# Reordering the pooling stage at the head of a two-layer trunk

## The chip, the cores and the metric

The kernel runs on one core of one Trainium2 chip. The metric is the device time of one launch in microseconds (us). The times shown of the kernel before are three runs: 983.19, 983.37 and 987.84 us, median 983.37. A profile is one execution, recorded by the chip's profiler. Its engines are PE (TensorE, matrix products), DVE (VectorE), ACT (ScalarE), POOL (GpSimd) and SP (SyncE, which here only issues DMAs).

## The reference

A decoder trunk of two layers on 512 tokens of width 1024, in float32:

```python
# layer 0: pooling mixer, layer 1: differential attention; each followed by a SwiGLU FFN
h = pool(x)                       # 4 groups of 256 columns, windows 2, 4, 8, 16
                                  # mixed = (mean over the last w tokens - x) @ w[g]; h = mixed * scale
x = LayerNorm(ALPHA * x + h)
x = LayerNorm(ALPHA * x + (silu(x @ w_gate) * (x @ w_up)) @ w_down)
```

`pool_w` is 4 x 256 x 256, `scale` has 1024 entries (one for each output column), `w_gate` and `w_up` are 1024 x 2816. The second layer does the same with attention in place of pooling. Only the first lines, the pooling mixer and its LayerNorm, are touched by the change.

## The kernel before

**Precision.** Float32 products are made of three faster ones: each operand is split in a high part (ACT casts it, L89) and a low part (DVE or POOL subtracts the cast from the original, L90), and `mm3` (L108 to L110) adds high x high, high x low and low x high in PSUM.

**Tiling.** The tokens are four blocks of 128. `res` holds x, a block in each of four column ranges; all sums and norms are made in it. The weights come as pieces of 128 x 1024 (512 KB) through a ring of four buffers `raw`; `fetch` issues their loads on SP's queue, `ready` splits them into `wh` and `wl` (rings of six). PSUM has eight banks, each a tile of 128 x 512.

**The pooling stage** (L217 to L402), in the order of the code:

1. Loads: the bands that pooling multiplies with (`bnd`, `d0`) on ACT's queue; x, the two pieces of pool weights, the scale row broadcast to 128 partitions (`sc`), the first FFN piece and small tables on SP's queue.
2. Nine warm-up matmuls on PE while x lands; then splits of x (`split_x`).
3. `low` pools blocks 0 and 1 into the banks of the first 256 tokens, `high` pools blocks 1, 2, 3 into those of the last 256. 40 and 48 matmuls of 256 columns.
4. `scale_weights` multiplies a piece of pool weights with `sc` (DVE, two instructions of 128 x 512), `pool_weights` splits it, `split_pooled` splits what was pooled, bank by bank.
5. `mixed(s)` multiplies block s with the pool weights (24 matmuls); `summed(s)` adds ALPHA * x and takes statistics (DVE: residual L145 and stats L152, twice); `spread_of` aggregates them (DVE, L158) and makes 1/sigma (POOL, two small instructions, L160 and L161); `norm` (DVE, L170) normalizes the block in place.
6. `turn(0, s)` transposes the block for the FFN: eight transposes on PE (L198), eight evictions on ACT with gain and bias (L203), two casts on ACT, and two low parts on DVE, whose row is `xt<-y,xt` at L90.

**Then the first FFN.** Its first two column tiles are computed for tokens 0 to 255 first (`g` and `u` products, 24 matmuls each), with `turn(0, 2)` and `turn(0, 3)` put in between, after the second and the third product; then for tokens 256 to 511.

**What sets the order.** The stage stands under `tc.manual_schedule()`. A helper's instructions are issued where it is called, each on the queue of its engine; the tile framework adds the semaphore waits and picks buffers.

Of the kernel before, what the change touches and what calls it, by code (L numbers as in the profile page):

```python
# [12 lines left out]
F32 = mybir.dt.float32  # L13
# [5 lines left out]
P = 128  # L19
S = 512  # L20
D = 1024
# [29 lines left out]
def trunk(ctx, tc, x, wall, pscale, lam_p, subln, table, lng, lnb, band, first, onehot, out):  # L51
    nc = tc.nc
# [5 lines left out]
    def bank(name):  # L58
        return ps.tile([P, 512], F32, tag="bank", name=name)
# [3 lines left out]
    def load_x(s):  # L63
        for d in range(2):
            c = slice(d * 512, (d + 1) * 512)
            nc.sync.dma_start(out=res[:, s, c], in_=x[s * P : (s + 1) * P, c])
# [8 lines left out]
    def fetch(upto):  # L75
        while fetched[0] < min(upto, total):
            c = fetched[0]
            raws[c] = keep.tile([P, 1024], F32, tag="raw", name=f"raw{c}", bufs=RAWS)
            nc.sync.dma_start(out=raws[c], in_=wall[c])
            fetched[0] += 1  # L80

    def split(dst_h, dst_l, src, scale=1.0, low=None):
        if scale != 1.0:
            nc.scalar.mul(dst_h, src, scale)
            nc.vector.scalar_tensor_tensor(
                dst_l, src, scale, dst_h.bitcast(F32), op0=ALU.mult, op1=ALU.subtract
            )
        else:
            nc.scalar.copy(dst_h, src)  # L89
            (low or nc.vector).tensor_tensor(dst_l, src, dst_h.bitcast(F32), op=ALU.subtract)  # L90

    def ready(upto, low=None):
        while divided[0] < min(upto, total):
            c = divided[0]
            fetch(c + RAWS)
            h = keep.tile([P, 1024], F32R, tag="wh", name=f"wh{c}", bufs=WBUFS)
            l = keep.tile([P, 1024], F32R, tag="wl", name=f"wl{c}", bufs=WBUFS)
            split(h, l, raws.pop(c), low=low)
            parts[c] = (h, l)
            divided[0] += 1  # L100
# [5 lines left out]
    def mm3(acc, a, b, start, stop):  # L106
        (ah, al), (bh, bl) = a, b
        nc.tensor.matmul(acc, ah, bh, start=start, stop=False)  # L108
        nc.tensor.matmul(acc, ah, bl, start=False, stop=False)  # L109
        nc.tensor.matmul(acc, al, bh, start=False, stop=stop)  # L110
# [81 lines left out]
    def turn(n, s):  # L192
        for i in range(2):
            pt = bank(f"pt{n}_{s}_{i}")
            y = keep.tile([P, 4, P], F32, tag="y", name=f"y{n}_{s}_{i}", bufs=2)
            for k in range(4):
                kk = 4 * i + k
                nc.tensor.transpose(  # L198
                    pt[:, k * P : (k + 1) * P], res[:, s, kk * P : (kk + 1) * P], ident
                )  # L200
            for k in range(4):
                kk = 4 * i + k
                nc.scalar.activation(  # L203
                    y[:, k, :],
                    pt[:, k * P : (k + 1) * P],
                    AF.Identity,
                    bias=bT[:, n, kk : kk + 1],
                    scale=gT[:, n, kk : kk + 1],
                )
            o = (s % 2) * P  # L210
            split(*(xt[:, s // 2, j, 4 * i : 4 * i + 4, o : o + P] for j in range(2)), y)
# [5 lines left out]
    with tc.tile_pool(name="pool", bufs=1) as pp:  # L217
        bnd = pp.tile([P, 4, 256], BF16, name="bnd")
        nc.scalar.dma_start(out=bnd, in_=band)
        d0 = pp.tile([16, 4, 16], F32, name="d0")  # L220
        nc.scalar.dma_start(out=d0, in_=first)
        for s in range(SB):
            load_x(s)
        fetch(1)
        sc = pp.tile([P, D], F32, name="sc")
        nc.sync.dma_start(out=sc, in_=pscale.broadcast_to([P, D]))
        fetch(3)
        tb = pp.tile([33, HEADS], F32, name="tb")
        nc.gpsimd.memset(tb, MASKED)
        nc.sync.dma_start(out=tb[:32, :], in_=table)  # L230
# [16 lines left out]
        def split_x(s, d, low=None):  # L247
            c = slice(d * 512, (d + 1) * 512)
            split(xnh[:, s, c], xnl[:, s, c], res[:, s, c], low=low)

        warm = bank("warm")
        for i in range(9):
            nc.tensor.matmul(warm[:, 0:P], ident, ident, start=True, stop=True)
        split_x(0, 0)
        nc.vector.tensor_copy(fh, bnd)
        split(fh[:16, :, 0:16], fl[:16, :, 0:16], d0)
# [2 lines left out]
        nc.scalar.copy(bh[:, :, P : 2 * P], bnd[:, :, :P])  # L259
        split_x(1, 1)  # L260
        nc.scalar.copy(bh[:, :, 2 * P : 3 * P], bnd[:, :, P:])
        ph = pp.tile([P, KB, S], F32R, name="ph")
        pl = pp.tile([P, KB, S], F32R, name="pl")
        pw = []

        def scale_weights(c):
            raw = raws[c]
            for j in range(2):
                r = raw[:, j * 512 : (j + 1) * 512].rearrange("p (k e) -> p k e", k=2)
                nc.vector.tensor_tensor(  # L270
                    r,
                    r,
                    sc[:, (2 * c + j) * GW : (2 * c + j + 1) * GW]
                    .unsqueeze(1)
                    .to_broadcast([P, 2, GW]),
                    op=ALU.mult,
                )

        def pool_weights(c):
            h = keep.tile([P, 1024], F32R, tag="wh", name=f"pwh{c}", bufs=WBUFS)  # L280
            l = keep.tile([P, 1024], F32R, tag="wl", name=f"pwl{c}", bufs=WBUFS)
            split(h, l, raws.pop(c))
            pw.append((h, l))
            divided[0] += 1
# [3 lines left out]
        def xk(t, s, k):  # L288
            return t[:, s, k * P : (k + 1) * P]
# [15 lines left out]
        def high(*blocks):  # L305
            for s in blocks:
                c = (3 - s) * P
                for k in range(KB):
                    g = k // 2
                    o = made[1, g][:, (k % 2) * 256 : (k % 2 + 1) * 256]  # L310
                    b = bh[:, g, c : c + 256]
                    mm(o, xk(xnh, s, k), b, start=s == 1 and k % 2 == 0, stop=False)
                    mm(o, xk(xnl, s, k), b, start=False, stop=s == 3 and k % 2 == 1)

        def split_pooled(half, *groups):
            for g in groups:
                c = slice(half * 256, (half + 1) * 256)
                split(
                    ph[:, 2 * g : 2 * g + 2, c],
                    pl[:, 2 * g : 2 * g + 2, c],  # L320
                    made[half, g].rearrange("p (k t) -> p k t", k=2),
                )

        def mixed(s):
            acc = [bank(f"mix{s}_{d}") for d in range(2)]
            for g in range(4):
                h, l = pw[g // 2]
                o = acc[g // 2][:, (g % 2) * GW : (g % 2 + 1) * GW]
                for k in range(2):
                    kk = 2 * g + k  # L330
                    c0 = (g % 2) * 512 + k * GW
                    mm3(
                        o,
                        (ph[:, kk, s * P : (s + 1) * P], pl[:, kk, s * P : (s + 1) * P]),
                        (h[:, c0 : c0 + GW], l[:, c0 : c0 + GW]),
                        k == 0,
                        k == 1,
                    )
            return acc
# [3 lines left out]
                residual(s, d, acc[d])  # L343
                stat(0, s, d)

        split_x(2, 0, nc.gpsimd)
        split_x(2, 1)
        split_x(3, 0, nc.gpsimd)
        split_x(3, 1)
        low(0, range(8))  # L350
        low(1, range(8))
        for g in range(4):
            made[1, g] = bank(f"pool1_{g}")
        high(1, 2)
        split_pooled(0, 0, 1)
        scale_weights(0)
        pool_weights(0)
        split_pooled(0, 2)
        scale_weights(1)
        pool_weights(1)  # L360
        split_pooled(0, 3)
        m0 = mixed(0)
        m1 = mixed(1)
        ready(3, nc.gpsimd)
        def lines_sum():
            b = [bank(f"line{i}") for i in range(2)]
            mm(b[0][:HEADS, :], tb, oh_[:, 0:512], start=True, stop=True)
            mm(b[1][:HEADS, :128], tb, oh_[:, 512:640], start=True, stop=True)
            return b

        high(3)
        summed(0, m0)
        spread_of(0, 0)
        split_pooled(1, 0, 1)
        norm(0, 0)
        ready(4, nc.gpsimd)
        summed(1, m1)
        spread_of(0, 1)
        split_pooled(1, 2, 3)
        norm(0, 1)  # L380
        turn(0, 0)
        b0, b1 = lines_sum()
        m2 = mixed(2)
        summed(2, m2)
        spread_of(0, 2)
        turn(0, 1)
        norm(0, 2)
        m3 = mixed(3)
        summed(3, m3)
        spread_of(0, 3)  # L390
        ready(5)
        norm(0, 3)
        ready(6)
        line = pp.tile([HEADS, LINE], F32, name="line")
        far = pp.tile([HEADS, 1], F32, name="far")
        nc.scalar.copy(far, b1[:HEADS, P - 1 : P])
# [682 lines left out]
```

## Time and profile before

| | us |
|---|---|
| median of three runs | 983.37 |
| profiled execution | 983.99 |
| its span | 982.1 |
| PE busy in the span | 960.4 |
| DVE / ACT / POOL busy | 641.3 / 418.3 / 120.4 |
| first pooling matmul starts | 6.96 |
| turn(0,0), turn(0,1) start on PE | 31.95, 37.09 |
| first FFN matmul starts | 40.84 |
| turn(0,2), turn(0,3) start on PE | 47.01, 50.76 |
| FFN's products for tokens 256 to 511 start | 54.51 |

How to read the rows. In a timeline a row is: start and duration in us, engine, line, operation, output<-inputs, shapes, xcount, and in brackets the idle time of the engine before it and what ended it. Merged rows show the start of the first and the time until the end of the last. Durations of PE's matmuls overlap: their starts are what counts. In the table by windows each row is: window, its length, then busy time and instruction count of PE, PEld (weight loads), DVE, ACT, POOL, then the clock that PE was granted (1.00 is full), the DMA engines' share and GB/s. A row of waits is: who waited, <- for whom, us in total, times, longest. A row of one tile's instructions gives the shortest, median and longest duration in ns and the first and last start. A row of DMA issues ends in KB and the median us from issue to landing.

### The profile page before, as it was taken

To read this page: it belongs to the slowest core of one execution; us is meant where nothing else is said; L and a number is where in the kernel's file an instruction comes from. 1 tells how busy PE (TensorE), PEld (TensorE's weight loads), DVE (VectorE), ACT (ScalarE), POOL (GpSimd) and SP (SyncE) were. 2 spreads that over 40 slices of the span, in tenths; PEclk is the share of its full clock that TensorE was granted. 3 is DMA by queue.
4 is the path that set the end of the run, shared out by engine and by line. 5 is a ranking of instruction groups with operands and counts; after the bars stand their busy time and mean duration, and the time that the engine had idled before them with its cause. 6 is when DMAs were issued, how large, how long until landed. Compare 5 with 4: busy or idle time off the path is not lost.

```text
span 982.1 us, 13302 instructions
## 1 busy us (share of the span) xinstructions
PE 960.4 (98%) x4922; PEld 815.5 (83%) x4922; DVE 641.3 (65%) x1007; ACT 418.3 (43%) x705; POOL 120.4 (12%) x192
## 2 busy tenths in 40 slices
PE   7999999999999999999999999999999999999995
PEld 6898888888888888988888888988888888888884
DVE  6756764455568577688777676756655555477687
ACT  4662222223326356656556554732223322245460
POOL 3301111111120211000000000011111111111102
PEclk8999999999999999999999999999999999999998
DMA  9266677655777975323232122276675666878842
GB/s 241 61 210 216 231 248 269 234 194 193 261 254 237 330 273 176 110 81 89 74 94 78 63 86 86 81 271 211 217 271 193 205 231 224 292 240 307 340 143 86
DMA packets 70221, 189.11 MB, mean 193 GB/s; under 512 B 15971, under 2 KB 16099, under 8 KB 70156
## 3 DMA queue, kind: packets, MB, share of 16 engines
q1 hardware_dynamic: 56556, 141.83, 43.0%
q0 software_dynamic: 13408, 46.15, 13.8%
q8 instruction: 39, 0.64, 0.3%
q10 hardware_dynamic: 192, 0.29, 0.1%
q14 instruction: 26, 0.21, 0.1%
HBM read 151.51 MB, written 36.72 MB: 192 GB/s over the span
## 4 chain that ended last, share of the span: by engine, by line
PE 86%; issue 5%; DVE 3%; ACT 2%; POOL 1%; DMA 1%; POOLq 0%; DVEq 0%
PE P L605 11%; PE g L109 8%; PE u L108 8%; PE u L109 8%; PE u L110 8%; PE g L108 8%; PE g L110 8%; PE Q L605 3%; PE s L790 2%; PE v L108 2%; PE v L109 2%; PE v L110 2%; PE wo L108 2%; PE wo L109 2%; PE wo L110 2%
## 5 line engine op out<-in xcount | busy, mean ns | idle before, releaser
L90 DVE TENSOR_TENSOR wl<-raw,wh 128x1024 fp32r<-128x1024 f32 x118 | 141.8, 1220 | 33.3 <-ACT wh L89 33.3
L89 ACT CAST wh<-raw 128x1024 fp32r<-128x1024 f32 x120 | 123.5, 1049 | 66.8 <-PE u L109 66.3
L109 PE MATMUL g<-xt,wh 128*128 128x512 f32 (+1 forms) x384 | 143.1, 373 | 0.5 <-DVE xt L90 0.3
L108 PE MATMUL g<-xt,wh 128*128 128x512 f32 (+1 forms) x384 | 143.0, 372 | 0.0
L108 PE MATMUL u<-xt,wh 128*128 128x512 f32 (+1 forms) x384 | 142.8, 372 | 0.0
L109 PE MATMUL u<-xt,wh 128*128 128x512 f32 (+1 forms) x384 | 142.8, 372 | 0.0
L110 PE MATMUL u<-xt,wl 128*128 128x512 f32 (+1 forms) x384 | 142.8, 372 | 0.0
L110 PE MATMUL g<-xt,wl 128*128 128x512 f32 (+1 forms) x384 | 142.7, 372 | 0.0
L436 DVE TENSOR_TENSOR hid<-sg,u 128x512 f32<-128x512 f32 x44 | 30.2, 687 | 155.8 <-PE u L110 153.5
L90 DVE TENSOR_TENSOR dl<-r,dh 128x1024 fp32r<-128x1024 f32 x84 | 94.2, 1132 | 39.9 <-ACT dh L89 39.5
L89 ACT CAST dh<-r 128x1024 fp32r<-128x1024 f32 x84 | 81.4, 979 | 71.7 <-PE P L605 31.2
L605 PE MATMUL P<-dh,xt 128*128 128x512 f32 x352 | 109.6, 390 | 0.0
L109 PEld LDWEIGHTS g<-xt,wh 128*128 128x128 f32 x384 | 72.3, 188 | 13.2 <-DVE xt L90 0.9
L110 PEld LDWEIGHTS u<-xt,wl 128*128 128x128 f32 x384 | 72.4, 189 | 12.5
L108 PEld LDWEIGHTS u<-xt,wh 128*128 128x128 f32 x384 | 72.4, 189 | 12.4
L110 PEld LDWEIGHTS g<-xt,wl 128*128 128x128 f32 x384 | 72.3, 188 | 12.5
L109 PEld LDWEIGHTS u<-xt,wh 128*128 128x128 f32 x384 | 72.4, 189 | 12.3
L108 PEld LDWEIGHTS g<-xt,wh 128*128 128x128 f32 x384 | 72.3, 188 | 12.4
L480 ACT CAST v<-u 128x512 fp32r<-128x512 f32 x22 | 13.6, 620 | 160.8 <-issue 151.1
L605 PEld LDWEIGHTS P<-dh,xt 128*128 128x128 f32 x352 | 66.1, 188 | 13.9 <-issue 0.2
L460 DVE TENSOR_TENSOR b<-b,b 128x512 f32<-128x512 f32 x88 | 60.8, 691 | 17.3 <-DMA b<-in_wall 15.2
L435 ACT ACTIVATE sg<-g 128x512 f32<-128x512 f32 x44 | 26.3, 598 | 101.0 <-PE g L110 99.3
(179 smaller groups left out, 1775.6 us busy)
## 6 DMA issues: line engine op xcount, KB each, us to landing
raw<-in_wall SPq DMA_DIRECT2D x128, 512.0 KB, 4.3
b<-in_wall SPq DMA_DIRECT2D x88, 256.0 KB, 5.6
tsum<-b POOLq DMA_DIRECT2D x88, 256.0 KB, 5.1
r<-tsum SPq DMA_DIRECT2D x40, 512.0 KB, 4.7
r<-in_wall SPq DMA_DIRECT2D x30, 512.0 KB, 4.7
ssum<-v POOLq DMA_DIRECT2D x22, 512.0 KB, 4.1
xt<-ssum POOLq DMA_DIRECT2D x20, 512.0 KB, 6.1
res<-in_x SPq DMA_DIRECT2D x8, 256.0 KB, 4.3
```

Source lines behind the costliest of these rows:

```text
L89: nc.scalar.copy(dst_h, src)
L90: (low or nc.vector).tensor_tensor(dst_l, src, dst_h.bitcast(F32), op=ALU.subtract)
L108: nc.tensor.matmul(acc, ah, bh, start=start, stop=False)
L109: nc.tensor.matmul(acc, ah, bl, start=False, stop=False)
L110: nc.tensor.matmul(acc, al, bh, start=False, stop=stop)
L435: nc.scalar.activation(sg, pg, AF.Silu)
L436: nc.vector.tensor_tensor(hid[:, f, :], sg, pu, op=ALU.mult)
L460: nc.vector.tensor_tensor(z, x, y, op=ALU.add)
L480: nc.scalar.copy(v[:, :, 0, :], u)
L605: nc.tensor.matmul(accs[s], x[:, k, r], y[:, c], start=first and k == 0 and e == 0, stop=last and k == m - 1 and e == 2, skip_group_check= ...
L790: nc.tensor.matmul(accs[c][:, :wide], a[r, qs], b[r, :wide], start=i == 0, stop=i == 2)
```

## The change

All of it is in the pooling stage.

- The scale row is loaded once (4 KB, on ACT's queue) and no longer broadcast by a DMA; two matmuls with a row of ones (`one`, set by POOL) spread it over 128 partitions in two banks, and ACT copies these into `sc`. Four of the nine warm-up matmuls go.
- The first FFN piece is fetched right behind the pool weights.
- POOL multiplies the pool weights with the scales; the low parts of blocks 2 and 3 that POOL made are made by DVE.
- `high` runs for blocks 1, 2, 3 in one stretch, ahead of all mixing; half of `split_pooled(1)` moves in front of the second pool weights' split, `ready(4)` stands in front of mixing.
- `turn(0, 0)` and the sums of the lines stand ahead of `mixed(2)` and of `summed(1)`; `turn(0, 1)` ahead of `summed(2)` and `mixed(3)`; `ready(5)` ahead of `norm(0, 1)`, `ready(6)` ahead of `norm(0, 3)`.

```diff
--- before.py
+++ after.py
@@ -217,14 +217,16 @@
     with tc.tile_pool(name="pool", bufs=1) as pp:
         bnd = pp.tile([P, 4, 256], BF16, name="bnd")
         nc.scalar.dma_start(out=bnd, in_=band)
+        scrow = pp.tile([1, D], F32, name="scrow")
+        nc.scalar.dma_start(out=scrow, in_=pscale)
         d0 = pp.tile([16, 4, 16], F32, name="d0")
         nc.scalar.dma_start(out=d0, in_=first)
         for s in range(SB):
             load_x(s)
-        fetch(1)
+        fetch(3)
         sc = pp.tile([P, D], F32, name="sc")
-        nc.sync.dma_start(out=sc, in_=pscale.broadcast_to([P, D]))
-        fetch(3)
+        one = pp.tile([1, P], F32, name="one")
+        nc.gpsimd.memset(one, 1.0)
         tb = pp.tile([33, HEADS], F32, name="tb")
         nc.gpsimd.memset(tb, MASKED)
         nc.sync.dma_start(out=tb[:32, :], in_=table)
@@ -249,8 +251,13 @@
             split(xnh[:, s, c], xnl[:, s, c], res[:, s, c], low=low)
 
         warm = bank("warm")
-        for i in range(9):
+        for i in range(5):
             nc.tensor.matmul(warm[:, 0:P], ident, ident, start=True, stop=True)
+        scb = [bank(f"sc{c}") for c in range(2)]
+        for c in range(2):
+            nc.tensor.matmul(
+                scb[c], one, scrow[:, c * 512 : (c + 1) * 512], start=True, stop=True
+            )
         split_x(0, 0)
         nc.vector.tensor_copy(fh, bnd)
         split(fh[:16, :, 0:16], fl[:16, :, 0:16], d0)
@@ -259,6 +266,8 @@
         nc.scalar.copy(bh[:, :, P : 2 * P], bnd[:, :, :P])
         split_x(1, 1)
         nc.scalar.copy(bh[:, :, 2 * P : 3 * P], bnd[:, :, P:])
+        for c in range(2):
+            nc.scalar.copy(sc[:, c * 512 : (c + 1) * 512], scb[c])
         ph = pp.tile([P, KB, S], F32R, name="ph")
         pl = pp.tile([P, KB, S], F32R, name="pl")
         pw = []
@@ -267,7 +276,7 @@
             raw = raws[c]
             for j in range(2):
                 r = raw[:, j * 512 : (j + 1) * 512].rearrange("p (k e) -> p k e", k=2)
-                nc.vector.tensor_tensor(
+                nc.gpsimd.tensor_tensor(
                     r,
                     r,
                     sc[:, (2 * c + j) * GW : (2 * c + j + 1) * GW]
@@ -343,54 +352,50 @@
                 residual(s, d, acc[d])
                 stat(0, s, d)
 
-        split_x(2, 0, nc.gpsimd)
-        split_x(2, 1)
-        split_x(3, 0, nc.gpsimd)
-        split_x(3, 1)
+        for i in range(4):
+            split_x(2 + i // 2, i % 2)
         low(0, range(8))
         low(1, range(8))
         for g in range(4):
             made[1, g] = bank(f"pool1_{g}")
-        high(1, 2)
-        split_pooled(0, 0, 1)
+        high(1, 2, 3)
         scale_weights(0)
+        scale_weights(1)
+        split_pooled(0, 0, 1, 2, 3)
         pool_weights(0)
-        split_pooled(0, 2)
-        scale_weights(1)
+        split_pooled(1, 0, 1)
         pool_weights(1)
-        split_pooled(0, 3)
-        m0 = mixed(0)
-        m1 = mixed(1)
         ready(3, nc.gpsimd)
+        ready(4, nc.gpsimd)
+
         def lines_sum():
             b = [bank(f"line{i}") for i in range(2)]
             mm(b[0][:HEADS, :], tb, oh_[:, 0:512], start=True, stop=True)
             mm(b[1][:HEADS, :128], tb, oh_[:, 512:640], start=True, stop=True)
             return b
 
-        high(3)
+        m0 = mixed(0)
+        m1 = mixed(1)
         summed(0, m0)
         spread_of(0, 0)
-        split_pooled(1, 0, 1)
+        split_pooled(1, 2, 3)
         norm(0, 0)
-        ready(4, nc.gpsimd)
+        b0, b1 = lines_sum()
+        turn(0, 0)
+        m2 = mixed(2)
         summed(1, m1)
         spread_of(0, 1)
-        split_pooled(1, 2, 3)
+        ready(5)
         norm(0, 1)
-        turn(0, 0)
-        b0, b1 = lines_sum()
-        m2 = mixed(2)
+        turn(0, 1)
         summed(2, m2)
         spread_of(0, 2)
-        turn(0, 1)
+        m3 = mixed(3)
         norm(0, 2)
-        m3 = mixed(3)
         summed(3, m3)
         spread_of(0, 3)
-        ready(5)
+        ready(6)
         norm(0, 3)
-        ready(6)
         line = pp.tile([HEADS, LINE], F32, name="line")
         far = pp.tile([HEADS, 1], F32, name="far")
         nc.scalar.copy(far, b1[:HEADS, P - 1 : P])
```

## The prediction

> **What bounds the kernel now.** Read first: the page's busy times, then PE's windows, then who waited for whom. All positions are us from the span's start.
>
> ```profile
> PE 960.4 (98%) x4922; PEld 815.5 (83%) x4922; DVE 641.3 (65%) x1007; ACT 418.3 (43%) x705; POOL 120.4 (12%) x192
> ```
>
> ```profile
> 6.96:15.70 8.74, 8.74 (x72) 8.58 (x72) 7.31 (x10) 5.59 (x11) 3.00 (x2) 1.00 1.11 332
> 15.70:18.46 2.76, 0.55 (x3) 0.19 (x1) 1.65 (x3) 1.53 (x2) 0.00 (x0) 1.00 0.87 11
> 18.46:28.50 10.04, 8.44 (x47) 7.85 (x48) 6.46 (x10) 2.48 (x3) 3.17 (x3) 0.66 0.77 210
> ...
> 30.40:31.95 1.55, 0.16 (x3) 0.03 (x1) 1.55 (x4) 1.55 (x3) 0.68 (x1) 1.00 0.00 0
> 31.95:40.84 8.89, 8.89 (x69) 7.82 (x69) 8.69 (x16) 7.45 (x20) 2.97 (x4) 1.00 0.18 61
> 40.84:54.51 13.67, 13.53 (x115) 13.33 (x113) 9.45 (x14) 10.71 (x25) 2.65 (x4) 1.00 0.44 154
> ```
>
> PE is 98% busy, so a change ahead of the first FFN can only move the moment at which PE's unbroken run begins. It begins at 31.95: from there PE is busy in 8.89 of 8.89 and 13.53 of 13.67. Before it PE stands 2.2 in 15.70:18.46, about 1.6 in 18.46:28.50 (which also ran at a granted clock of 0.66), and 1.4 in 30.40:31.95. Those stalls are all that a better order can win.
>
> ```profile
> ACT ph L89 <- PE pool L313: 6.5, 1, 6.5
> ```
>
> The third block's pooling stands behind two blocks of mixing, so ACT waits 6.5 for it, and DVE's norm and PE's first turn (pt) come late. PE ran these matmuls at 28.50 although their inputs were split at 13.67 (rows below) and PE stood idle at 16: each queue keeps the order of the code.
>
> **The part that gains: up to the first turn.** The row of scales and its two matmuls first.
>
> ```profile
> 2.33 3.91 PE L253 MATMUL warm<-ident 128*128 128x128 f32 x18 [2.33 <-POOL ident masks.py:199]
> ...
> 32.94 1.02 PE L367 MATMUL line<-oh__105,tb 33*8 33x512 f32 x2
> 33.80 0.38 PE L368 MATMUL line<-oh__105,tb 33*8 33x128 f32 x2
> ```
>
> ```profile
> d<-in_first ACTq DMA_DIRECT2D x1, 4.0 KB, 4.0
> ```
>
> ```profile
> 9.42 2.18 ACT L89 CAST xt<-res 128x512 fp32r<-128x512 f32 x4
> ...
> 29.17 1.07 ACT L89 CAST ph<-pool 128x512 fp32r<-128x512 f32 x2 [6.45 <-PE pool L313]
> ```
>
> Four warm-up matmuls (8 of 18 records) go: -1.7. The row of scales is issued on ACT's queue where d was (1.16) and, like d, should land 4.0 later, at 5.2. No K=1 matmul is in the trace; the nearest row, 33 x 512, holds PE from 32.94 to 33.80, 0.86, so two cost +1.7, or +3.4 at half clock. Pooling starts between 6.96, as now, and 8.6. ACT's two copies of scales are sized like the ph casts: 1.07, so its casts of blocks 2 and 3 end at 12.7, not 11.6.
>
> Now Pool's multiplications, against DVE's splits of blocks 2 and 3, all four now on DVE:
>
> ```profile
> 10.12 3.00 POOL L90 TENSOR_TENSOR xt<-res,xt 128x512 fp32r<-128x512 f32 x2 [6.91 <-ACT xt L89]
> ...
> 10.59 3.08 DVE L90 TENSOR_TENSOR xt<-res,xt 128x512 fp32r<-128x512 f32 x2 [0.87 <-ACT xt L89]
> ```
>
> ```profile
> L90 DVE TENSOR_TENSOR xt<-res,xt x6: 684/693/1773, 5.3 to 11.9; 128x512 fp32r<-128x512 f32 x6
> L90 POOL TENSOR_TENSOR xt<-res,xt x2: 1307/1522/1736, 10.1 to 11.4; 128x512 fp32r<-128x512 f32 x2
> ```
>
> ```profile
> 22.80 2.38 POOL L90 TENSOR_TENSOR wl<-raw,wh 128x1024 fp32r<-128x1024 f32 x1 [9.68 <-ACT wh L89]
> ...
> 23.07 0.68 DVE L145 SCALAR_TENSOR_TENSOR res<-res,mix 128x512 f32<-128x512 f32 x1
> ```
>
> ```profile
> raw<-in_wall SPq DMA_DIRECT2D x1, 512.0 KB, 5.5
> ...
> sc<-in_pscale SPq DMA_DIRECT2D x1, 512.0 KB, 6.5
> ```
>
> Alone DVE's takes 0.69 and Pool's 1.31; side by side they took 1.77 and 1.74, each ending about 0.5 and 1.25 after the other: they take turns, 1.75 a pair. A DVE instruction with one operand in PSUM (23.07, during Pool's 22.80) keeps its 0.68. The first weights, issued at 5.70, land at 11.2; the broadcast of scales behind them, issued at 6.18, lands at 12.7, so without it what follows it on SP's queue can land 1.5 sooner. Four Pool multiplications against four DVE splits, from 11.2: DVE's last split ends near 16.95 (13.67 now), Pool's last near 18.2. Bounds: no taking of turns gives 13.4 and 16.3.
>
> Then in DVE's order, at 0.61 per pooled split and 1.2 per weight split: four pooled splits to 19.35, first weights to 20.55, two pooled splits to 21.75. Pool's split of the next piece (2.38) takes 20.55 to 22.85 in between, so the second weights end at 23.95. PE has pooled everything by 17.6 to 19.3 (88 matmuls at 0.12, the 72 in 8.74 of the first window), so its start costs nothing here; without that cover it would cost at most 1.7. Mixing 0 ends near 25.4. Residuals, stats, rs and norm follow:
>
> ```profile
> 29.79 1.29 DVE L90 TENSOR_TENSOR pl<-pool,ph 128x512 fp32r<-128x512 f32 x2 [2.78 <-ACT ph L89]
> 31.00 0.80 DVE L170 TENSOR_SCALAR res<-res,mv,rs 128x1024 f32<-128x1024 f32 x1
> 31.72 0.68 DVE L145 SCALAR_TENSOR_TENSOR res<-res,mix 128x512 f32<-128x512 f32 x1
> ...
> 34.48 0.21 DVE L158 BATCH_NORM_AGGREGATE mv<-st 128x2 f32<-128x12 f32 x1
> ```
>
> ```profile
> 27.11 0.22 POOL L160 TENSOR_SCALAR rs<-mv 128x1 f32<-128x1 f32 x1 [1.93 <-DVE mv L158]
> 27.41 0.57 POOL L161 TENSOR_TENSOR rs<-rs,mhalf 128x1 f32<-128x1 f32 x1
> ```
>
> The second residual starts at 25.45 and its stats and the aggregate end at 27.1; Pool's rs 0.95 and two pooled splits 1.2 side by side; norm 0.8: done at 29.0, against 31.8. PE mixes block 1 until 28.3, sums the lines (1.1) and turns block 0 at 29.4 against 31.95. **Gain 2.55.** If DVE and Pool don't take turns, norm ends at 27.1, and the turn is at 27.25: rs then stands in Pool's queue behind two weight splits, the second of a piece that is issued behind bT.
>
> ```profile
> 9.56 7.08 SPq L234 DMA_DIRECT2D bT<-in_lnb  x1
> 16.69 31.03 SPq L79 DMA_DIRECT2D raw<-in_wall  x6
> ```
>
> ```profile
> raw<-in_wall SPq DMA_DIRECT2D x1, 512.0 KB, 6.7
> ```
>
> That piece lands 6.7 after 16.69, at 23.4, and 1.5 sooner without the broadcast, 21.9; the cast takes 1.05, Pool 2.4, rs 0.95, norm 0.8: 27.1.
>
> **The part that loses: from the first turn to the last.** turn() ends in two DVE subtractions, and turn(0,0) now stands ahead of summed(1), turn(0,1) ahead of summed(2). DVE, which keeps its order, must stand until ACT has evicted the turn. Behind it wait the residual, the norm, and PE's next turn.
>
> ```profile
> 31.95 1.07 PE L198 MATMUL pt<-ident,res 128*128 128x128 f32 x8 [1.39 <-DVE res L170]
> ...
> 37.09 1.04 PE L198 MATMUL pt<-ident,res 128*128 128x128 f32 x8
> ...
> 41.97 0.70 DVE L90 TENSOR_TENSOR xt<-y,xt 128x512 fp32r<-128x512 f32 x1 [0.77 <-ACT xt L89]
> ...
> 46.06 0.21 DVE L158 BATCH_NORM_AGGREGATE mv<-st 128x2 f32<-128x12 f32 x1
> 46.18 1.18 DVE L90 TENSOR_TENSOR wl<-raw,wh 128x1024 fp32r<-128x1024 f32 x1
> ...
> 48.13 0.81 DVE L170 TENSOR_SCALAR res<-res,mv,rs 128x1024 f32<-128x1024 f32 x1 [0.77 <-POOL rs L161]
> ...
> 50.76 1.03 PE L198 MATMUL pt<-ident,res 128*128 128x128 f32 x8
> ...
> 56.01 0.69 DVE L90 TENSOR_TENSOR xt<-y,xt 128x512 fp32r<-128x512 f32 x1 [1.36 <-ACT xt L89]
> ...
> 56.76 0.39 PE L109 MATMUL g<-xt,wh 128*128 128x256 f32 x1 [0.34 <-DVE xt L90]
> ```
>
> The pieces: a turn from PE's start to DVE's last subtraction, 37.09 to 42.67, 5.58; a sum from residual to aggregate, 31.72 to 34.69, 2.97; aggregate to norm with a weight split between (ready(5) now as ready(6) before), 46.27 to 48.13, 1.86, and without it 1.0; norm 0.81; norm to turn 0.15. New chain:
>
> - turn(0,0) 29.4 + 5.58 + 2.97 + 1.86 + 0.81 + 0.15 = turn(0,1) at 40.8, against 37.09. PE has mixed block 2 by 33.2 and stands 7.6.
> - turn(0,1) + 5.58 + 0.45 (its first four transposes at half clock) + 2.97 + 1.0 + 0.81 (norm 2) + 2.97 + 1.86 + 0.81 + 0.15 = 16.6: turn(0,3) at 57.4, against 50.76.
>
> In between PE does turn(0,1) (0.8), three FFN products and mixing 3 (24 matmuls of 0.12, 2.9 each) and turn(0,2) (0.8), 13.2 at full clock: it would be there at 54.0, so DVE's chain sets turn(0,3). **Loss 6.6, less 0.35** (the last turn now waits for ACT's eviction of turn(0,2), 56.01 + 0.69 being 5.94 after its start; that wait goes). Net +6.25. From the FFN's second half on PE's work is unchanged.
>
> The other edits are hidden: the third small load on ACT's queue (its first cast waits for x, at 4.69), Pool's memset of ones, and the weight loads behind pool weights that come free 1 to 2 later (not used before 40.84).
>
> PE ran at a clock of 0.66 in 18.46:28.50 after standing in 15.70:18.46, which is half clock for 6.8 of the 10.04, and 7.6 is a longer stand. If that returns behind turn(0,1), PE reaches turn(0,3)'s place 3.4 later, at 57.4, still not later than DVE.
>
> The Trainium skill says (TensorE: Matmul & The Clock Gate, Part 1) that after about one idle window of 3.4 us PE drops to half rate and needs a busy window to recover. By that rule the slowdown behind turn(0,1) is certain; the trace agrees in kind (0.66 above). The sum would stay the same by it unless the stand before turn(0,3) brings a second one, which is the third rival.
>
> **Sum.** The profiled execution took 983.99 (span 982.1 and 1.9 around it); +6.25 makes 990.2. The median shown, 983.37, is 0.6 lower: 989.6.
>
> **Rivals.**
>
> 1. Pool and DVE don't get in each other's way (ACT's casts space DVE's splits out, or Pool's broadcast operand leaves room). For: only one meeting of the two shows it. Against: both rows there doubled. Turn(0,0) at 27.25, 2.15 earlier, +4.1: 987.5.
> 2. Not slower: the front gains more than the chain loses. It decides at turn(0,0): the chain grows from 18.8 (31.95 to 50.76) to 28.0, so the kernel is not slower if that turn starts before 23.1. For: all stalls and the half clock go when pooling is in one stretch. Against: rs behind the fourth piece, which would have to land at 18, near its issue at 16.69. 983.4.
> 3. Clock: PE stands at turn(0,1) and again about 1 to 2 before turn(0,3); two windows in part idle grant half clock while the FFN already runs, where PE is the bound. 6.8 at half clock costs 3.4 more: 993.0. For: the 0.66 stretch. Against: 30.40:31.95, 1.4 of standing, stayed at 1.00.
> 4. The code's order is not the queues' order (a planner puts summed(1) ahead of the subtractions). Turn(0,1) then follows norm 0 at 29.0 by 5.8, at 34.8, 2.3 earlier than now: 981.1. Against: the pooling at 28.50.
>
> **Chances.** Forecast 0.60, rivals 0.14, 0.07, 0.13, 0.06. About 0.5%, 4.9 us, is what a measurement of this kernel can tell from no change: slower begins at 988.3. A fifth of the forecast's weight lies below that (turn(0,0) 1.2 earlier). Slower: 0.48 + 0.13 = 0.61; same: 0.12 + 0.14 + 0.07 + 0.03 = 0.36; faster 0.03. The range runs from rival 1 with a piece that lands 2 sooner (985.5) to just past rival 3 (993.2); the forecast's own from 987.8 to 991.2 (mixing 0 and 1 at half clock, +1.1, and a late scale row).
>
> **What would show it.** DVE idle some 4 to 5 in two pieces between norm(0,0) and summed(1), ended by ACT's casts, and again ahead of summed(2); a PE gap of 6 to 8 in front of turn(0,1) with a clock of 0.5 behind it; the split of block 3 ending past 16; turn(0,0) at 28 to 30 and turn(0,3) at 56 to 58.5. The forecast is wrong if turn(0,1) starts before 37, if DVE runs summed(1) ahead of turn(0,0)'s subtractions, or if DVE's splits keep 0.69 beside Pool.

## The result, and the profile after

The changed kernel takes 990.54 us (median of six runs, 989.40 to 991.50). The kernel before, run beside it on the same chip, takes 985.69 (six runs, 983.19 to 987.84). The ratio is 1.0052, with a 95% interval of 1.0034 to 1.0070: slower by half a per cent. Profiled execution against profiled execution the loss is larger, 990.38 against 983.99, +6.4. The medians differ by only 4.85, because the later runs of the kernel before lay higher than its profiled one; in the later comparisons its median was 984.56, 985.13 and 985.34.

The page of the changed kernel, busy times. PE's sum has grown by 3.9 us, although it has four matmul records fewer, so most of the loss looks like PE's clock and not like waiting; the stage table shows that it is both.

```profile
PE 964.3 (98%) x4918; PEld 816.6 (83%) x4918; DVE 639.5 (65%) x1005; ACT 419.8 (42%) x707; POOL 124.9 (13%) x195
```

The windows of the changed kernel by stage; the columns are the window, its length, busy time and count of PE, PEld, DVE, ACT and POOL, the granted clock, the DMA share and GB/s.

```profile
8.13:20.00 11.87, 11.87 (x87) 11.87 (x87) 8.62 (x12) 8.33 (x16) 6.68 (x4) 1.00 0.93 176
20.00:28.90 8.90, 7.68 (x58) 6.39 (x56) 7.08 (x11) 4.09 (x6) 5.66 (x4) 1.00 0.77 260
28.90:33.00 4.10, 3.93 (x32) 3.72 (x32) 0.69 (x1) 3.40 (x9) 0.00 (x0) 1.00 0.19 75
33.00:40.20 7.20, 0.00 (x0) 0.03 (x1) 5.38 (x8) 1.69 (x3) 1.65 (x2) 0.69 0.08 17
40.20:46.00 5.80, 5.80 (x28) 5.80 (x29) 1.12 (x2) 4.61 (x11) 0.00 (x0) 0.50 0.65 254
```

The pooling runs in one stretch (its first matmul starts at 8.13, its last ends at 20.50, and PE has no gap in the first row), as the change says. The stall has moved: PE does nothing at all for 7.2 us in 33.00:40.20, and then works for 5.8 us at a clock of 0.50.

PE's timeline of the changed kernel shows the three turns that matter (start, duration, count, and in brackets the idle time before and what ended it):

```profile
28.90 1.06 PE L198 MATMUL pt<-ident,res 128*128 128x128 f32 x8 [0.83 <-DVE res L170]
...
40.20 1.94 PE L198 MATMUL pt<-ident,res 128*128 128x128 f32 x8 [7.38 <-DVE res L170]
...
56.66 1.06 PE L198 MATMUL pt<-ident,res 128*128 128x128 f32 x8 [0.39 <-DVE res L170]
...
62.32 0.39 PE L109 MATMUL g<-xt,wh 128*128 128x256 f32 x1 [0.17 <-DVE xt L90]
```

Against the kernel before, turn(0,0) starts 3.05 earlier (28.90 for 31.95), turn(0,1) 3.11 later (40.20 for 37.09), turn(0,3) 5.90 later (56.66 for 50.76), and the first FFN product behind the last turn 5.56 later (62.32 for 56.76). So 5.56 of the 6.4 is there before the first FFN has all its blocks.

DVE's timeline of the changed kernel shows why. Both stands of DVE in front of a turn's subtraction (xt<-y,xt) are ended by ACT, and the residual, the stats and the norm of the next block stand behind them in DVE's queue:

```profile
27.94 0.81 DVE L170 TENSOR_SCALAR res<-res,mv,rs 128x1024 f32<-128x1024 f32 x1 [1.08 <-POOL rs L161]
31.75 0.69 DVE L90 TENSOR_TENSOR xt<-y,xt 128x512 fp32r<-128x512 f32 x1 [3.00 <-ACT xt L89]
33.81 0.69 DVE L90 TENSOR_TENSOR xt<-y,xt 128x512 fp32r<-128x512 f32 x1 [1.36 <-ACT xt L89]
34.42 0.68 DVE L145 SCALAR_TENSOR_TENSOR res<-res,mix 128x512 f32<-128x512 f32 x1
...
37.18 0.21 DVE L158 BATCH_NORM_AGGREGATE mv<-st 128x2 f32<-128x12 f32 x1
37.30 1.18 DVE L90 TENSOR_TENSOR wl<-raw,wh 128x1024 fp32r<-128x1024 f32 x1
39.24 0.81 DVE L170 TENSOR_SCALAR res<-res,mv,rs 128x1024 f32<-128x1024 f32 x1 [0.76 <-POOL rs L161]
43.52 0.69 DVE L90 TENSOR_TENSOR xt<-y,xt 128x512 fp32r<-128x512 f32 x1 [3.46 <-ACT xt L89]
```

DVE stood 4.36 between norm(0,0) and the residual of block 1, although PE had mixed that block before it began turn(0,0).

### The profile page after: what moved, and what is told of

It is laid out like the page before. It is cut to its first block, busy times and chain, and to the rows that moved or that the text cites. A ratio compares the mean times of both kernels' runs of the same rounds, so it can differ in the third digit from the quotient of the medians.

```text
span 988.6 us, 13297 instructions
## 1 busy us (share of the span) xinstructions
PE 964.3 (98%) x4918; PEld 816.6 (83%) x4918; DVE 639.5 (65%) x1005; ACT 419.8 (42%) x707; POOL 124.9 (13%) x195
## 4 chain that ended last, share of the span: by engine, by line
PE 84%; issue 5%; DVE 3%; DMA 2%; ACT 2%; POOL 2%; SPq 1%; POOLq 0%; DVEq 0%
PE P L610 11%; PE u L108 8%; PE u L110 8%; PE u L109 8%; PE g L109 8%; PE g L110 8%; PE g L108 8%; PE Q L610 3%; PE s L795 2%; PE v L108 2%; PE v L109 2%; PE v L110 2%; PE wo L108 2%; PE wo L109 2%; PE wo L110 2%
## 5 line engine op out<-in xcount | busy, mean ns | idle before, releaser
L110 PEld LDWEIGHTS g<-xt,wl 128*128 128x128 f32 x384 | 72.4, 188 | 12.5
L465 DVE TENSOR_TENSOR b<-b,b 128x512 f32<-128x512 f32 x88 | 60.8, 691 | 19.3 <-DMA b<-in_wall 17.1
```

Of the source, the lines that this page charges most:

```text
L465: nc.vector.tensor_tensor(z, x, y, op=ALU.add)
```

## Experiments

### The two halves of the change, one at a time

The first kernel keeps all of the change but puts the turns back to where they were:

```
 norm(0, 0)
-b0, b1 = lines_sum()
-turn(0, 0)
-m2 = mixed(2)
 summed(1, m1)
 spread_of(0, 1)
-ready(5)
 norm(0, 1)
-turn(0, 1)
+turn(0, 0)
+b0, b1 = lines_sum()
+m2 = mixed(2)
 summed(2, m2)
 spread_of(0, 2)
+turn(0, 1)
...
```

> The changed kernel with the turns (and ready(5), ready(6), the sums of the lines) back in the order of before; the early pooling, POOL's scaling and the spread by matmuls stay. Theory (DVE stands behind the turns' subtractions): turn(0,0) stays at 28.9 and the chain from it to turn(0,3) is 18.8 again instead of 27.8, so turn(0,3) near 47.7, some 9 us ahead of the changed kernel: about 3 us under the kernel before, ratio 0.997. Rival (the loss lies in POOL's scaling, the port or the clock at the head): as slow as the changed kernel, ratio about 1.005.

The second keeps the kernel before and moves only the turns (ready(5) and ready(6) stay at the end, as before):

```
 ready(4, nc.gpsimd)
-summed(1, m1)
-spread_of(0, 1)
 split_pooled(1, 2, 3)
-norm(0, 1)
 turn(0, 0)
 b0, b1 = lines_sum()
 m2 = mixed(2)
+summed(1, m1)
+spread_of(0, 1)
+norm(0, 1)
+turn(0, 1)
 summed(2, m2)
 spread_of(0, 2)
-turn(0, 1)
...
```

> The kernel before with nothing but the turns ahead of the next sums (turn(0,0) ahead of summed(1), turn(0,1) ahead of summed(2)); the head is untouched. Theory: turn(0,0) at 31.95 as before, turn(0,1) near 42.5 (37.1 before), turn(0,3) near 58.5 (50.8 before), about 7.7 us slower, ratio 1.008; PE stands some 5 to 7 us in front of turn(0,1). Rival (the loss lies at the head): within 1 us of before.

Measured: the turns alone take 993.46, a ratio of 1.0084 (1.0068 to 1.0101) to the kernel before. With the turns back the kernel takes 984.86, a ratio of 0.9997 (0.9985 to 1.0010). The moved turns therefore cost the whole loss: 8.9 on top of the kernel before (984.56 beside it), and 5.7 on top of the rest of the change (990.54 less 984.86, which were not run side by side; by the two ratios it is 5.4). DVE's and PE's timelines with the turns alone repeat the picture:

```profile
36.81 0.69 DVE L90 TENSOR_TENSOR xt<-y,xt 128x512 fp32r<-128x512 f32 x1 [1.36 <-ACT xt L89]
37.42 0.68 DVE L145 SCALAR_TENSOR_TENSOR res<-res,mix 128x512 f32<-128x512 f32 x1
```

```profile
31.90 1.06 PE L198 MATMUL pt<-ident,res 128*128 128x128 f32 x8 [1.39 <-DVE res L170]
...
42.35 1.94 PE L198 MATMUL pt<-ident,res 128*128 128x128 f32 x8 [5.14 <-DVE res L170]
...
59.86 1.03 PE L198 MATMUL pt<-ident,res 128*128 128x128 f32 x8
```

From turn(0,0) to turn(0,3) it takes 27.96 here and 27.76 in the changed kernel, against 18.81 before. DVE's order sets that length, whatever lies ahead of it.

The first kernel missed its expectation: its turn(0,0) starts at 28.99, 2.96 earlier than in the kernel before, but its turn(0,3) starts at 50.90 (47.7 was expected, the kernel before has 50.76), and nothing is won. PE's windows (window, length, busy and count, granted clock, DMA share, GB/s) and timeline of the kernel with the turns back:

```profile
28.00:30.00 2.00, 1.01 (x6) 0.82 0.79 252
30.00:32.00 2.00, 2.00 (x6) 0.50 0.03 10
32.00:34.00 2.00, 2.00 (x8) 0.50 0.00 0
34.00:36.00 2.00, 2.00 (x12) 0.50 0.00 0
36.00:38.00 2.00, 2.00 (x18) 0.97 0.00 0
```

```profile
28.99 1.66 PE L198 MATMUL pt<-ident,res 128*128 128x128 f32 x8 [1.93 <-DVE res L170]
```

A stand of 1.93 in front of that turn is followed by some 6.8 us at half clock (about 29.3 to 36.1, worked out from the clock of the windows; the matmuls' spacing goes back from 0.21 to 0.12 at 36.16). They cost some 3.4, about the 3 that the turn had come earlier. The clock would thus explain why the earlier pooling was worth nothing. Of the twelve executions one, with a mean clock of 0.996, took 980.72; the others, at 0.991 to 0.993, took 983.88 to 987.37, which fits. The reading is tested further down, by taking the stand away.

### What holds the front: scale row, Pool's multiplications, warm-up

Four kernels change only the front. In the first, DVE scales the weights and not Pool:

```
-nc.gpsimd.tensor_tensor(r, r, sc[...], ...)
+nc.vector.tensor_tensor(r, r, sc[...], ...)
```

> The changed kernel with the pool weights scaled by DVE instead of POOL. If POOL's four multiplications (12.5 to 19.2) hold the head up, mixing 0's second half starts earlier than 22.4 and turn(0,0) earlier than 28.9, by 1 us or more. If PE's pooling at half clock holds it up (it ends at 19.0, and ACT's casts of it, the second pool weights' cast and DVE's splits follow in order), turn(0,0) stays within 0.5 us of 28.9.

The second has nine warm-up matmuls for five:

```
-for i in range(5):
+for i in range(9):
     nc.tensor.matmul(warm[:, 0:P], ident, ident, start=True, stop=True)
```

> The changed kernel with nine warm-up matmuls instead of five, the two K=1 matmuls behind them. If PE's clock came late (11.9 instead of 5.7) because the warm-up was too short and had a gap, full clock now comes by about 8.5, pooling ends 1 to 1.5 us earlier than 19.0, and turn(0,0) comes up to 0.9 us earlier (POOL's last multiplication ends at 19.2 and is then the later one). If the K=1 matmuls themselves don't count as work for the clock, full clock comes no earlier than about 11 and nothing moves.

The third brings the scales by the old broadcast DMA and keeps Pool's multiplications:

```
-scrow = pp.tile([1, D], F32, name="scrow")
-nc.scalar.dma_start(out=scrow, in_=pscale)
...
-fetch(3)
+fetch(1)
+nc.sync.dma_start(out=sc, in_=pscale.broadcast_to([P, D]))
+fetch(3)
...
+for i in range(9):     # and no scb matmuls, no copies of them
```

> The changed kernel with the scales spread by the broadcast DMA and nine warm-up matmuls, the two K=1 matmuls and ACT's copies gone; POOL's scaling and the turns' order stay. If the K=1 matmuls keep the clock at half: full clock by 8, pooling ends near 17.6. POOL's scaling starts when the broadcast lands, near 13, and ends near 19.5, so turn(0,0) gains at most 0.5 us on 28.9; turn(0,1) follows 11.3 behind it as before.

The fourth spreads the scales with matmuls of 128 rows, of which one holds the scales and the others zeros:

```
-scrow = pp.tile([1, D], F32, name="scrow")
+scrow = pp.tile([P, D], F32, name="scrow")
+nc.gpsimd.memset(scrow, 0.0)
...
-one = pp.tile([1, P], F32, name="one")
+one = pp.tile([P, P], F32, name="one")
...
+for i in range(11):
```

> The changed kernel with the spread done by full 128-row matmuls (ones of 128 x 128 against a tile that is zero but for the scale row) and eleven warm-up matmuls, so that PE has no gap ahead of them. If the clock's gate counts only how long PE is busy, nothing changes against the run with nine warm-ups (full clock at 13.9). If it counts how many rows work, full clock comes by about 9, while the spreading matmuls still run.

Measured, one execution each: 990.45, 991.84, 990.41 and 990.21. Three are as slow as the changed kernel (990.54), and the one with nine warm-ups lies above all six of its runs. None of these parts explains the loss. Their traces still settle what the prediction said of them.

In the changed kernel itself the spread takes 3.77, and the pooling behind it begins at half pace, one matmul every 0.21, until 11.9 (0.12 from there on; the clock column reads 1.00 at this place, so the spacing is what shows it). PE's timeline of the changed kernel:

```profile
4.42 3.77 PE L258 MATMUL sc<-scrow,one 1*128 1x512 f32 x4 [0.39 <-DMA scrow<-in_pscale]
...
11.28 0.41 PE L309 MATMUL pool<-fh,xt 128*128 128x256 f32 x1
11.49 0.41 PE L307 MATMUL pool<-fh,xt 128*128 128x256 f32 x1
...
11.90 0.28 PE L309 MATMUL pool<-fh,xt 128*128 128x256 f32 x1
12.02 0.28 PE L307 MATMUL pool<-fh,xt 128*128 128x256 f32 x1
```

And with nine warm-ups, where PE has no gap from 1.52 on and still comes to full pace only at 14.0:

```profile
1.52 4.21 PE L255 MATMUL warm<-ident 128*128 128x128 f32 x18 [1.52 <-POOL tb L231]
5.66 3.78 PE L258 MATMUL sc<-scrow,one 1*128 1x512 f32 x4
...
13.80 0.41 PE L309 MATMUL pool<-fh,xt 128*128 128x256 f32 x1
14.02 0.33 PE L307 MATMUL pool<-fh,xt 128*128 128x256 f32 x1
```

With nine warm-ups the pooling ends at 22.18 instead of 20.50, and turn(0,0) comes at 30.51, 1.61 later than in the changed kernel; "nothing moves" was the expectation. With the broadcast DMA full pace comes at 7.3 and the pooling ends 2.95 sooner (17.55), but turn(0,0) comes only 0.13 sooner (28.77), and turn(0,1), after a stand of 7.36, at 40.07. With DVE scaling, full pace comes later than in the changed kernel (13.9), although warm-up and spread are the same; the pooling ends at 21.24, 0.74 later, and turn(0,0) comes 0.69 later (29.59). That run therefore does not show what Pool's scaling costs; the four splits of blocks 2 and 3 took 2.50 in it. With 128 rows the spread took 1.88 at 6.36 and the pooling ended at 18.57, but DVE's four splits took 4.69 and its split of the second weights 3.30 beside Pool's work, and turn(0,0) came at 29.70.

So a later pooling delays the first turn almost in full, and an earlier one hardly brings it forward. Two waits in ACT's timeline of the changed kernel show why:

```profile
19.10 1.08 ACT L89 CAST ph<-pool 128x512 fp32r<-128x512 f32 x2 [2.35 <-PE pool L322]
...
23.53 1.05 ACT L89 CAST wh<-raw 128x1024 fp32r<-128x1024 f32 x1 [1.46 <-DMA raw<-in_wall]
```

The first wait is for the pooling. Behind that cast stand, in ACT's queue, the casts of the second pool weights and of the third weight piece (ready(3)), and Pool's split of that piece starts behind them, at 22.15. The second wait is for the fourth piece (ready(4)), which was issued at 16.56. Its cast ends at 24.58, and Pool comes to its split at 24.66. The pooling and the fourth piece thus arrive level, to 0.1 us: with the broadcast DMA the cast of the fourth piece still started at 23.41. The slow start cost the changed kernel only some 0.1, but it left no room.

### Where the gain of the earlier pooling went

What holds norm(0,0) in the changed kernel is Pool's order: rs stands behind two splits of weight pieces, ready(3) and ready(4), although the aggregate that it needs ended at 25.71. POOL's timeline of the changed kernel:

```profile
12.51 6.68 POOL L279 TENSOR_TENSOR raw<-raw,sc 128x512 f32<-128x512 f32 x4 [9.16 <-ACT xt L89]
22.15 4.91 POOL L90 TENSOR_TENSOR wl<-raw,wh 128x1024 fp32r<-128x1024 f32 x2 [2.96 <-ACT wh L89]
27.02 0.23 POOL L160 TENSOR_SCALAR rs<-mv 128x1 f32<-128x1 f32 x1
```

So the next kernel takes the one with the turns back, moves ready(4) behind norm(0,0), and the sum of the lines into the place where PE stood:

```
 ready(3, nc.gpsimd)
-ready(4, nc.gpsimd)
...
 norm(0, 0)
+ready(4, nc.gpsimd)
 summed(1, m1)
 spread_of(0, 1)
 norm(0, 1)
-turn(0, 0)
 b0, b1 = lines_sum()
+turn(0, 0)
```

> The early pooling with the turns' old order (as in the run with the turns put back), and PE's stand in front of turn(0,0) filled: the sums of the lines stand ahead of turn(0,0), and the split of the fourth piece (ready(4)) behind norm(0,0), so that POOL's rs need not wait for it. The run with the turns put back stood 1.9 us in front of turn(0,0) and then ran at half clock for 6.8 us, which is worth 3.4. Theory (that half clock ate the gain of the early pooling): PE stands 1 us or less there, the clock stays at 1.00, turn(0,3) at 46 to 48, ratio 0.994 to 0.997. Rival (early pooling gains nothing, the head's end is fixed by something else): ratio 0.999 to 1.001.

Measured: 982.58, a ratio of 0.9975 (0.9966 to 0.9984). It is faster, but not as meant: the stand did not go. DVE's and POOL's timelines of this kernel, and its first turn:

```profile
27.34 2.75 DVE L170 TENSOR_SCALAR res<-res,mv,rs 128x1024 f32<-128x1024 f32 x1
```

```profile
27.20 2.34 POOL L90 TENSOR_TENSOR wl<-raw,wh 128x1024 fp32r<-128x1024 f32 x1
```

```profile
30.24 1.89 PE L198 MATMUL pt<-ident,res 128*128 128x128 f32 x8 [1.61 <-DVE res L170]
```

Pool's split started 0.14 before the norm, and the norm, 0.81 elsewhere, took 2.75: it ended 0.55 after Pool did. PE stood 1.61, and its clock read 0.58 and 0.57 in the next two windows of 2 us. From turn(0,0) to turn(0,3) (49.27) it still took only 19.03, as the sum of the lines, 1.1 of PE's work, now lies ahead of turn(0,0).

One more step moves ready(4) behind turn(0,0), so that Pool's split no longer meets the norm:

```
 norm(0, 0)
-ready(4, nc.gpsimd)
...
 turn(0, 0)
+ready(4, nc.gpsimd)
 m2 = mixed(2)
```

> As the run in which PE's stand was to be filled (early pooling, the turns' old order, the sums of the lines first), with the fourth piece's split issued behind turn(0,0) instead of behind norm(0,0). In that run POOL's split started right when rs was done and norm(0,0) took 2.75 instead of 0.8. Theory (DVE and POOL take turns at a port): norm(0,0) takes 0.8 again, turn(0,0) comes near 28.5 instead of 30.2, PE stands 0.5 us or less in front of it and the clock stays at 1.00: ratio 0.993 to 0.996. Rival (norm was long for another reason): norm(0,0) above 2 again, ratio 0.997 to 0.998.

Measured: **981.17, a ratio of 0.9960 (0.9947 to 0.9973)** to the kernel before (985.34 beside it): the version that beats both. Its norm, its turns, and PE's windows:

```profile
27.64 0.81 DVE L170 TENSOR_SCALAR res<-res,mv,rs 128x1024 f32<-128x1024 f32 x1
```

```profile
28.54 0.38 PE L373 MATMUL line<-oh__108,tb 33*8 33x128 f32 x2
28.85 1.09 PE L198 MATMUL pt<-ident,res 128*128 128x128 f32 x8
...
33.28 1.06 PE L198 MATMUL pt<-ident,res 128*128 128x128 f32 x8 [0.47 <-DVE res L170]
...
47.64 1.03 PE L198 MATMUL pt<-ident,res 128*128 128x128 f32 x8
```

```profile
28.00:30.00 2.00, 2.00 (x14) 1.00 0.14 57
30.00:32.00 2.00, 2.00 (x19) 1.00 0.00 0
32.00:34.00 2.00, 1.53 (x14) 1.00 0.00 0
```

PE goes from the lines into turn(0,0) without a stand, and the clock stays at 1.00. The turns take 18.79 from first to fourth, the 18.81 of before, and the first and the fourth come 3.1 earlier. That is the gain which the kernel with the turns put back had at its first turn and had lost by its last. That the half clock goes when the stand goes is shown; how much of the 3.1 is the clock's is not, since the sum of the lines, which now fills the wait, was moved in the same step. The median fell by 4.2; the other 1.1 was not followed. The ratio is at the upper end of what was expected.

Two kernels add the broadcast DMA, nine warm-ups and DVE's scaling to these two, which ends the pooling some 3.5 us sooner (17.6 and 17.7 for 21.1 and 21.3):

> As the run before it in this list, with the scales spread by the broadcast DMA and nine warm-up matmuls as in the kernel before, and the pool weights scaled by DVE. Theory (the K=1 matmuls hold PE's clock back to 12 or 14 and cost 3.8 of PE themselves): full clock by 8, pooling ends near 17.6 instead of 19.0, turn(0,0) about 1 us earlier than in the run before it, ratio 0.993 to 0.996. Rival (the head is bound by DVE and ACT, not by PE's pooling): within 0.3 us of the run before it at turn(0,0).

> The same move of the fourth piece's split in the run with the broadcast DMA, nine warm-ups and DVE's scaling. Theory: norm(0,0) takes 0.8 instead of 2.77, turn(0,0) near 29.9 (the lines end at 29.9 there), PE stands nowhere behind 23; the half clock from 23 to 27 stays, since the second pool weights' split still waits for POOL's split of the third piece (2.51 instead of 1.23). Ratio 0.995 to 0.998, 0.5 to 1.5 us behind the other kernel of this list.

Measured: 982.77, a ratio of 0.9978 (0.9968 to 0.9988), and with ready(4) behind turn(0,0) 982.45, 0.9972 (0.9963 to 0.9981). Neither is better than its pair. The second came as expected; the first met neither theory nor rival, as its turn(0,0) came 0.47 later than in its pair. PE now waits for the second pool weights, whose split again meets one of Pool's. PE's and DVE's timelines of the first of the two:

```profile
19.12 0.39 PE L109 MATMUL mix<-pwl,ph 128*128 128x256 f32 x1 [1.43 <-DVE pwl L90]
...
22.76 0.39 PE L109 MATMUL mix<-pwl,ph 128*128 128x256 f32 x1 [1.93 <-DVE pwl L90]
```

```profile
20.19 2.51 DVE L90 TENSOR_TENSOR pwl<-raw,pwh 128x1024 fp32r<-128x1024 f32 x1
```

Half clock follows once more (0.58 and 0.57 in 23 to 27), and turn(0,0) comes at 30.71 and 29.92. In these two an earlier pooling does not reach the first turn: the second weights' split and the half clock take the gain. In the best kernel (981.17) it might. There PE's own work sets turn(0,0): full pace came only at 14.1, the pooling ended at 21.33, and from it PE runs through mixing and lines into the turn with one stand of 0.41, while the norm is done at 28.45. A kernel that spreads the scales by DMA and also keeps Pool's split of the third piece away from the second weights' was not tried.

## Why the prediction was right

The forecast, slower with 989.6 for a median of 990.54, came out, from turn to turn by its own chain, at the front by another path. Step by step:

- **The loss from turn to turn: right.** Turn(0,0) to turn(0,1) was forecast at 11.37 and took 11.30; turn(0,1) to turn(0,3) at 16.6 and took 16.46. The pieces agree: 28.90 to 34.50 for the turn (5.60), 34.42 to 37.39 for the sum (2.97), 1.85 from aggregate to norm. PE stood 7.38 (7.6 forecast). That DVE's order is the cause is shown by the two halves above: moved alone, the turns cost as much (27.96 for 27.76 from first to fourth turn), and put back, the loss is gone.
- **The gain of the front: right in size, by errors that cancel.** Turn(0,0) was forecast at 29.4 and came at 28.90, so the gain was 3.05 and not 2.55, but another path set it. The forecast let PE's own work set the turn (mixing until 28.3, then 1.1 for the lines, with the norm done at 29.0). In the run PE had done the lines at 28.07 and stood 0.83 for the norm, which ended at 28.75. Pool's and DVE's taking of turns was over-sized: Pool began when two of DVE's four splits were over, and only the fourth met a multiplication, so the four took 3.59 (2.50 where DVE scales) and ended at 14.51, not 16.95. The second weights ended at 22.39, not 23.95, and the aggregate at 25.71, not 27.1. Pool's own four took 6.68 (7.0 forecast), but began at 12.51, not 11.2, because the first weights needed 6.3 to land. Against that, norm(0,0) waited for rs behind two of Pool's splits (4.91, end 27.06). The prediction priced that queue only in its first rival, and there let the fourth piece land at 21.9 and the norm end at 27.1; the piece's cast, which waited for it, began at 23.53.
- **The spread by matmuls: too cheap, and only just hidden.** The pair was put at 1.7, or 3.4 at half clock; it took 3.77 and left the pooling at half pace until 11.9, which no step had named. The pooling ended at 20.50 for the forecast's 17.6 to 19.3. That the start costs nothing held (with the pooling 2.95 sooner, turn(0,0) moved by 0.13), but the cover had no room: with the pooling 1.68 later, the turn came 1.61 later.
- **The last turn's shorter wait: right**, 0.34 (56.66 to 62.32 is 5.66, before 6.00) for 0.35.
- **The clock behind the stand: right.** It read 0.50 from 36 to 46, and PE, forecast to be at turn(0,3) no later than DVE, stood there 0.39. The Trainium skill (TensorE: Matmul & The Clock Gate, Part 1) has PE fall to half rate after about one idle window of 3.4 us, and the trace agrees for this stand of 7.38. The stands of 1.61 and 1.93 above brought half clock as well, and there the measurement decides against taking 3.4 as a lower limit.
- **From the FFN's second half on unchanged: nearly.** Of the 6.4, 5.56 is there at 62.32 and 5.5 at the first matmul of P (320.3 for 314.8). Another 0.9 arises before v (399.8 for 393.4). Its cause stays open; it is less than single runs of the kernel before differ by (983.19 to 987.84).

The net up to 62.32 came to 5.56 where 6.25 was forecast: a gain too small by 0.5 and a chain too long by 0.2 both made the forecast too slow, and a late 0.9, which it did not have, made up for it. In the medians the loss is 4.85, 1.4 less than forecast. That 989.6 lies within 1 us of 990.54 is thus in part luck: the sum started from 983.37, the median of three runs of the kernel before, of which six gave 985.69.

**The rivals.** Pool and DVE do get in each other's way (first rival), though for one of the four splits (1.78 for 0.69); at turn(0,0) the trace lies between forecast and rival, nearer to the forecast (28.90, for 29.4 and 27.25). The front did not gain enough to carry the turns (second): that needed 23.1, and no kernel here had turn(0,0) before 28.77. A second half-clock stretch (third) did not come, as PE stood only 0.39. The queues kept the order of the code (fourth).

## What to carry to other kernels

An engine that keeps its order pays for a round trip written into it early: before a step is pulled forward, list what stands behind its last instruction on each engine, and add up the chain to the next such step. Here that addition from rows of the old trace gave the time from the first turn to the last to 0.2 us in 28. A gain won ahead of PE can be lost again to a stand of under 2 us if the clock falls behind it, so read the granted clock next to each wait, and look for the work (here the sum of the lines, and one weight split moved by a few lines) that closes the gap. And ask of each part that is called hidden how much room its cover has: the pooling here had 0.1 us.

## What the runs showed of the hardware

- **Behind matmuls with one row PE came to full pace late.** With nine warm-ups PE was busy from 1.52 to 14.0, 12.5 us without a gap, and yet at half pace throughout; the 3.78 with one row stand in the middle. In the kernel before, 3.91 of warm-up was enough for full pace at 7.5. The six kernels with the one-row spread came to full pace between 11.9 and 14.2, the five without any spread by matmuls between 7.2 and 7.5, and the one with 128 rows by 8.2. With 128 rows the spread itself took 1.88, but there the pace may have risen during the eleven warm-ups ahead of it, so the number of rows is the likeliest cause and not a proven one.
- **A short stand can bring half clock, and does not always.** 1.61 and 1.93 in front of turn(0,0) were followed by some 3.4 and 6.8 us of it; 1.4 at the same place in the kernel before was not, nor 0.83 in the changed one. Nor were 1.60 in front of turn(0,3) (broadcast DMA, nine warm-ups) and 1.86 in front of an FFN product (turns alone, at 57.12): the clock read 1.00 for the 8 us behind each. So the length of a stand alone does not decide. In the kernel with 1.61, PE had summed the lines before it (1.2, of 33 rows by 8 columns), which may count as little work; what does decide was not tried.
- **DVE and Pool shut each other out for a whole instruction.** The norm took 2.75 (and 2.77) for 0.81, the weights' split 2.51 for 1.21, each time with a split of Pool's of 2.34 to 2.38 under way; the norms ended 0.55 after Pool's split, the weights' split 1.08 after it. The Trainium skill (SBUF — State Buffer, SBUF: two separate sides) says that the two share one pair of ports as an exclusive lock held for the whole instruction; these rows agree with it.
